# A gathered block's input fetched half a block ahead, its residual mid-way, and the final norms of the dense blocks interleaved

## The chip, the cores and the metric

The kernel runs on one core of a Trainium2 chip. The core has five engines with instruction streams of their own: TensorE (PE, matrix products into PSUM), VectorE (DVE), ScalarE (ACT), GpSimd (POOL) and SyncE (SP), which here only issues DMAs. The metric is the device time of one execution in microseconds. It is read from three runs of the kernel before: a median of 2697.93 us (2694.83 to 2700.26).

## The reference, cut to what matters

One layer of a streaming encoder over 1024 tokens of width 1024, in float32. A token mixer comes first (not touched here). Then follows a retrieval over 128 x 128 = 16384 single-neuron experts, and a final norm:

```python
def peer_ffn(x, wq, k1, k2, u_tab, v_tab):
    def block(xb):                      # 128 tokens
        ...                             # 8 heads, each picks its 16 best experts: e, softmax weights g
        u_sel = u_tab[e]
        act = jax.nn.gelu(jnp.einsum('thkd,td->thk', u_sel, xb))
        v_sel = v_tab[e]
        return jnp.einsum('thk,thkd->td', g * act, v_sel)
...
    h = h + peer_ffn(rms_norm(h, norm2_g[l]), ...)
return rms_norm(h, normf_g)             # x * rsqrt(mean(x*x) + 1e-6) * g
```

Each token uses 8 x 16 = 128 experts. Per block of 128 tokens one can gather the 128 rows of `u_tab` and of `v_tab` that each token needs, or multiply with all 16384 experts and weigh by a mostly zero matrix.

## The kernel before, in words

The eight token blocks are divided: five (numbers 0 to 4, `ND`) go the dense way on PE, three (`NG`) the gathered way on DVE, at the same time.

**Dense blocks.** `first` computes gelu(u x) for one column of 128 experts and all 640 tokens (tiles `ap`, `aa`, `ha`); 97 such columns are computed ahead and stored to the DRAM tensor `A_d`. The weights are built as `G_d` and loaded as `gt`. The loop `dense` then goes over 32 groups of four columns. In each it loads `hr` (from `A_d`), `vr` and `ur`, weighs (`weigh`), splits values into a high and a low part (`hh`, `hl`, `vh`, `vl`, `uh`, `ul`; high on ACT, low on DVE) and multiplies on PE: 24 matmuls of width 512 for each token block. Blocks 0 to 3 go to accumulators `vp` (PSUM, two buffers, taken by `pair`) and are added to the residual on DVE by `add`; block 4 stays in the accumulator `total` over all groups. The next buffer of `vp` is free only when its `add` is done.

**Gathered blocks.** `gather(n)` is a generator. It loads the block's normalized input `xg` from DRAM (`X_d`) and forms 128 dot products on DVE, one for each gathered row of `u` (the instruction shown as CUSTOM_DVE, `row<-row,xg`). Then it loads the residual `hb` (from `H_d`), applies gelu, and adds 128 weighted rows of `v` to it (SCALAR_TENSOR_TENSOR, `hb<-row,act,hb`). `finish` norms the result and stores it. Rows are gathered by POOL into a ring of eight buffers; `xg`, `hb` and `act` have one buffer each.

**What sets the order.** In front of the dense loop a planner (`Merge`) interleaves generators by estimated costs, and the scheduler of the language places DMAs on SP where their buffers come free. The dense loop is written out by hand (`manual_schedule`): `rows_of(slot)` draws a fixed share of gathered rows at seven places of each group. SP issues in program order, so a DMA that waits holds back all later ones.

**The end.** The last group does block 0 and block 1; then `last` does blocks 2, 3 and 4. Each block's `finish` norms it: a square with a sum on ACT, a root on ACT, five one-column operations on DVE (`rsqrt_cols`), a load of the norm's weights `nf` for all partitions, one multiply on DVE and one store.

Most instructions are recorded through a helper and carry its line, 146; they are told apart by their tiles. DMA issues carry their own lines: 1254 `xg`, 1262 `hb`, 1278 `nf`, 1283 the output, 1318 `hr`, 1322 `vr`, 1382 the store of `A_d`, 1424 `gt`.

Of the kernel before, what the change touches and what calls it, by code (L numbers as in the profile page):

```python
# [7 lines left out]
F32 = mybir.dt.float32  # L8
# [939 lines left out]
def peer(tc, a, cst, pools, h, nx, mg):  # L948
# [299 lines left out]
    def gate():  # L1248
        return (lambda: mg.units < share[0]) if share else None

    def gather(n):

        xg = gp.tile([P, D], F32, name="xg", tag="xg", bufs=1)
        nc.sync.dma_start(xg, X_d[n])
        act = gp.tile([P, P], F32, name="act", tag="act", bufs=1)
        for k in range(P):
            ub = take()
            yield gate()
            V.tensor_tensor_reduce(ub, ub, xg, 1.0, 0.0, ALU.mult, ALU.add, act[:, k:k + 1])
            mg.units += 1  # L1260
        hb = gp.tile([P, D], F32, name="hb", tag="hb", bufs=1)
        nc.sync.dma_start(hb, H_d[n])
        S.activation(act, act, AF.Gelu_apprx_tanh)
        yield
        V.tensor_tensor(act, act, gw[n], ALU.mult)
        yield
        for k in range(P):
            vb = take()
            yield gate()
            V.scalar_tensor_tensor(hb, vb, act[:, k:k + 1], hb, ALU.mult, ALU.add)  # L1270
            mg.units += 1
        finish(ND + n, hb)
        yield
# [172 lines left out]
        while mg.units < 2 * NG * P and left - (2 * NG * P - mg.units) + 1 <= spread[0]:  # L1446
            row()

    def second(p_, b, t, first, last):
        bs = slice(b * P, b * P + P)  # L1450
        for i in range(2):
            ns = slice(512 * i, 512 * i + 512)
            PE.matmul(p_[:, i], t.hh[:, bs], t.vl[:, ns], start=first, stop=False)
            PE.matmul(p_[:, i], t.hl[:, bs], t.vh[:, ns], start=False, stop=False)
# [5 lines left out]
    def pair():  # L1460
        return ppv.tile([P, 2, 512], F32, name="vp", tag="vp")
# [72 lines left out]
    def dense():  # L1534
# [3 lines left out]
        for c in range(nch):  # L1538
# [32 lines left out]
                second(pr[1], 1, t, jj == 0, jj == JC - 1)  # L1571
            add(0, pr[0])
            if not more:
                finish(0, acc[0])
            rows_of(2)
            if not more:
                last(now, pr)
                return

            pr.append(pair())  # L1580
            for jj, t in enumerate(now):
# [33 lines left out]

    def last(now, pr):

        for b in (2, 3, 4):
            p_ = pair() if b < 4 else total
            for jj, t in enumerate(now):  # L1620
                second(p_, b, t, b < 4 and jj == 0, jj == JC - 1)
            if b == 2:
                add(1, pr[1])
                finish(1, acc[1])
            else:
                add(b - 1, p0)
                finish(b - 1, acc[b - 1])
            p0 = p_
        add(4, total)
        finish(4, acc[4])  # L1630

    with tc.manual_schedule():
        dense()
# [81 lines left out]
```

## Time and profile before

| what | value |
|---|---|
| median of three runs | 2697.93 us (2694.83 to 2700.26) |
| the profiled execution's own time | 2685.19 us |
| its span, first to last instruction | 2683.4 us |
| mean granted PE clock | 0.974 |
| busy: PE, DVE, ACT, POOL | 94%, 88%, 50%, 44% of the span |
| DMA | 755.39 MB, mean 282 GB/s |

The span has three parts: the mixer and the choice of experts (to about 700 us), the building of the weights beside the columns computed ahead (to about 1550 us), and the dense loop with its end. In a row of the timeline stand the start in us, the duration, the engine, the operation with its output and inputs, and in brackets the idle time before it with what ended it. Rows `PE` are matmuls, whose ends are modelled. In a chain's row stand the start, the length and what was waited for or done.

### The profile page before, as it was taken

How to read it: one execution, taken by the hardware profiler on the slowest of the kernel's cores; microseconds unless marked ns; L12 is line 12 of the kernel's file. 1: busy time of each engine (PE TensorE's matmuls, PEld its weight loads, DVE VectorE, ACT ScalarE, POOL GpSimd, SP SyncE). 2: the span in 40 equal slices, each digit the busy share in tenths (PEclk: the TensorE clock that was granted, in tenths of full speed). 3: DMA queues.
4: the chain of work that ended last, by engine and by line, in shares of the span. 5: the costliest groups of instructions: out<-in, count | busy, mean ns of one | idle time of the engine just before them, and what ended most of it. 6: DMA issues, size and time to landing. Idle time of an engine off the chain costs nothing.

```text
span 2683.4 us, 40720 instructions
## 1 busy us (share of the span) xinstructions
PE 2517.4 (94%) x14623; PEld 2276.8 (85%) x14623; DVE 2364.5 (88%) x4541; ACT 1330.2 (50%) x2408; POOL 1172.7 (44%) x777
## 2 busy tenths in 40 slices
PE   5989899998999999999899889999899999999997
PEld 5766688998999999999899878888788888888885
DVE  6888649998999999999899779999888888999996
ACT  5457524322693965938739544444334333333432
POOL 0000000155573767847637535554444545555440
PEclk9989899999999999999999899999999999999998
DMA  5111324488899998999989989999899999999993
GB/s 169 32 35 37 126 80 127 147 281 313 275 401 317 354 392 306 396 341 357 401 276 364 388 321 331 332 328 323 291 329 326 330 324 329 333 329 327 329 330 133
DMA packets 298250, 755.39 MB, mean 282 GB/s; under 512 B 28352, under 2 KB 122752, under 8 KB 293312
## 3 DMA queue, kind: packets, MB, share of 16 engines
q0 software_dynamic: 110592, 402.70, 41.6%
q1 hardware_dynamic: 180720, 338.90, 35.6%
q10 hardware_dynamic: 6736, 11.19, 1.2%
q8 instruction: 115, 1.88, 0.3%
q14 instruction: 87, 0.71, 0.1%
HBM read 665.54 MB, written 85.98 MB: 280 GB/s over the span
## 4 chain that ended last, share of the span: by engine, by line
PE 60%; DVE 21%; DMA 9%; ACT 6%; issue 4%; ACTq 0%; SPq 0%; POOL 0%; DVEq 0%; POOLq 0%
PE vp L146 25%; PE ap L146 17%; PE total L146 6%; DMA A_d<-aa 4%; PE qp L146 4%; ACT ohB L146 3%; PE gp L146 3%; PE wop L146 3%; DVE row L146 2%; DVE oh L146 2%; DVE ul L146 2%; PE pj L146 2%; DVE hb L146 1%; DVE ix L146 1%; DMA nf<-in_gf_dram 1%
## 5 line engine op out<-in xcount | busy, mean ns | idle before, releaser
L1233 POOL DMA_INDIRECT row<-in_peer_u_dram,idx x384 | 562.6, 1465 | 961.0 <-DVE scv L146 495.6
L1233 POOL DMA_INDIRECT row<-in_peer_v_dram,idx x384 | 607.3, 1581 | 448.0 <-DVE hb L146 328.8
L146 PE MATMUL ap<-xDl,uh 128*128 128x320 f32 x2048 | 655.4, 320 | 30.5 <-ACT aa L146 23.9
L146 PE MATMUL ap<-xDh,ul 128*128 128x320 f32 x2048 | 648.0, 316 | 8.5 <-DVE ul L146 8.5
L146 PE MATMUL ap<-xDh,uh 128*128 128x320 f32 x2048 | 645.8, 315 | 0.0
L146 DVE SCALAR_TENSOR_TENSOR hb<-row,act,hb 128x1024 f32<-128x1024 f32 x384 | 492.3, 1282 | 8.9 <-DMA row<-in_peer_v_dram,idx 4.5
L146 DVE CUSTOM_DVE_ANT_0 row<-row,xg 128x1024 f32<-128x1024 f32 x384 | 458.4, 1219 | 15.4 <-DMA row<-in_peer_u_dram,idx 7.8
L146 PEld LDWEIGHTS ap<-xDl,uh 128*128 128x128 f32 x2048 | 392.5, 192 | 34.7 <-ACT aa L146 26.5
L146 PE MATMUL vp<-vl,hh 128*128 128x512 f32 x1024 | 400.7, 391 | 12.4 <-DVE vl L146 10.8
L146 PEld LDWEIGHTS ap<-xDh,ul 128*128 128x128 f32 x2048 | 392.3, 192 | 12.2 <-DVE ul L146 10.6
L146 PE MATMUL vp<-vh,hl 128*128 128x512 f32 x1024 | 399.9, 391 | 0.0
L146 PE MATMUL vp<-vh,hh 128*128 128x512 f32 x1024 | 399.6, 390 | 0.0
L146 PEld LDWEIGHTS ap<-xDh,uh 128*128 128x128 f32 x2048 | 391.7, 191 | 0.0
L146 ACT ACTIVATE gq<-gt 128x640 f32<-128x640 f32 x128 | 175.1, 1368 | 330.9 <-DVE hr L146 325.2
L146 DVE TENSOR_TENSOR ul<-ur,uh 128x1024 fp32r<-128x1024 f32 x128 | 155.9, 1218 | 97.3 <-ACT uh L146 97.2
L146 PEld LDWEIGHTS vp<-vl,hh 128*128 128x128 f32 x1024 | 193.0, 189 | 53.4 <-DVE vl L146 11.6
L146 PEld LDWEIGHTS vp<-vh,hh 128*128 128x128 f32 x1024 | 193.1, 189 | 40.5
L146 PEld LDWEIGHTS vp<-vh,hl 128*128 128x128 f32 x1024 | 193.2, 189 | 38.8
L146 PE MATMUL gp<-ohB,ohA 128*128 128x128 f32 x1280 | 198.1, 281 | 18.8 <-ACT gs L146 12.0
L146 ACT ACTIVATE aa<-ap 128x320 f32<-128x320 f32 x194 | 84.5, 437 | 258.8 <-PE ap L146 207.0
L146 ACT ACTIVATE ohB<-ohB,kt 128x128 f32<-128x128 f32 x480 | 204.4, 497 | 0.0
L146 PEld LDWEIGHTS gp<-ohB,ohA 128*128 128x128 f32 x1280 | 179.7, 193 | 24.4 <-ACT gs L146 13.3
(440 smaller groups left out, 4498.3 us busy)
## 6 DMA issues: line engine op xcount, KB each, us to landing
ur<-in_uT_dram SPq DMA_DIRECT2D x128, 512.0 KB, 6.7
vr<-in_peer_v_dram SPq DMA_DIRECT2D x128, 512.0 KB, 6.2
gt<-G_d SPq DMA_DIRECT2D x32, 1280.0 KB, 9.7
G_d<-gs SPq DMA_DIRECT2D x19, 2048.0 KB, 25.6
A_d<-aa SPq DMA_DIRECT2D x96, 320.0 KB, 8.6
hr<-A_d SPq DMA_DIRECT2D x96, 320.0 KB, 5.9
wqr<-in_wq_dram SPq DMA_DIRECT2D x31, 512.0 KB, 3.9
row<-in_peer_u_dram,idx POOLq DMA_INDIRECT x384, 7.2
```

What stands on the lines that cost most here:

```text
L146: return fn(*args, **kw)
L1233: G.indirect_dma_start(out=r, out_offset=None, in_=a["peer_v" if at >= P else "peer_u"], in_offset=bass.IndirectOffsetOnAxis(ap=idx[n][:, ...
```

## The change

Two separate edits.

In `gather`, the input `xg` of block n + 1 is fetched right behind the 128 dot products of block n, half a block ahead of its use, and handed over in a list; only block 0 still fetches its own. The residual `hb` is fetched behind the 65th dot product of its block, not behind the last.

In `last`, the norms of the five dense blocks become generators which are advanced in turns. The norm's weights `nf` are loaded once. The square of block b (ACT) is issued as soon as block b is added, and the rest of block b's norm comes after the next block's addition. Block 4's matmuls are issued by halves of the output: all of the first 512 columns, then all of the second. Its addition, its square (now on DVE, with a running sum) and its last multiply and store are done by halves. The last multiply of block 3 and its store come after those of block 4.

```diff
     def gather(n):
-        xg = gp.tile([P, D], F32, name="xg", tag="xg", bufs=1)
-        nc.sync.dma_start(xg, X_d[n])
+        xg = fetch_xg(n) if n == 0 else held.pop()
         act = gp.tile([P, P], F32, name="act", tag="act", bufs=1)
         for k in range(P):
             ub = take()
             yield gate()
             V.tensor_tensor_reduce(ub, ub, xg, 1.0, 0.0, ALU.mult, ALU.add, act[:, k:k + 1])
             mg.units += 1
-        hb = gp.tile([P, D], F32, name="hb", tag="hb", bufs=1)
-        nc.sync.dma_start(hb, H_d[n])
+            if k == P // 2:
+                hb = gp.tile([P, D], F32, name="hb", tag="hb", bufs=1)
+                nc.sync.dma_start(hb, H_d[n])
+        if n + 1 < NG:
+            held.append(fetch_xg(n + 1))
         S.activation(act, act, AF.Gelu_apprx_tanh)
...
-    def second(p_, b, t, first, last):
+    def second(p_, b, t, first, last, halves=(0, 1)):
         bs = slice(b * P, b * P + P)
-        for i in range(2):
+        for i in halves:
...
             add(0, pr[0])
             if not more:
-                finish(0, acc[0])
-            rows_of(2)
-            if not more:
                 last(now, pr)
                 return
+            rows_of(2)
...
     def last(now, pr):
+        nf = rows.tile([P, D], F32, name="nf", tag="row")
+        nc.sync.dma_start(nf, a["gf"].partition_broadcast(P))
+        def norm(b):
+            st = gp.tile([P, 5], F32, name="st4", tag="st4", bufs=2)
+            sq = rows.tile([P, D], F32, name="sqf", tag="row")
+            x = acc[b]
+            if b < 4:
+                S.activation(sq, x, AF.Square, accum_out=st[:, 2:3])
+                yield
+            else:
+                for i in range(2):
+                    xi = x[:, 512 * i:512 * i + 512]
+                    V.tensor_tensor(xi, xi, total[:, i], ALU.add)
+                    V.tensor_tensor_reduce(sq[:, 512 * i:512 * i + 512], xi, xi, 1.0, 0.0, ALU.mult, ALU.add,
+                                           st[:, i:i + 1])
+                    yield
+                V.tensor_tensor(st[:, 2:3], st[:, 0:1], st[:, 1:2], ALU.add)
+            v, dst = st[:, 3:4], st[:, 4:5]
+            V.tensor_scalar(v, st[:, 2:3], 1.0 / D, EPS, ALU.mult, ALU.add)
+            S.activation(dst, v, AF.Sqrt)
+            yield
+            V.reciprocal(dst, dst)
...
+            yield
+            n = 1 if b < 4 else 2
+            for i in range(n):
+                ns = slice(D // n * i, D // n * (i + 1))
+                V.scalar_tensor_tensor(x[:, ns], x[:, ns], dst, nf[:, ns], ALU.mult, ALU.mult)
+                nc.sync.dma_start(out_v[:, b, ns], x[:, ns])
+        g = [norm(b) for b in range(5)]
+        next(g[0])
+        rows_of(2)
+        p0 = pr[1]
+        for b in (2, 3):
+            p_ = pair()
             for jj, t in enumerate(now):
...
+            add(b - 1, p0)
+            next(g[b - 1])
+            for _ in g[b - 2]:
+                pass
             p0 = p_
+        for jj, t in enumerate(now):
+            second(total, 4, t, False, jj == JC - 1, (0,))
+        add(3, p0)
+        next(g[3])
+        for _ in g[2]:
+            pass
+        for jj, t in enumerate(now):
+            second(total, 4, t, False, jj == JC - 1, (1,))
+        next(g[4])
+        next(g[3])
+        next(g[4])
+        next(g[4])
+        next(g[3])
+        next(g[4])
+        for n in (4, 3):
+            for _ in g[n]:
+                pass
```

How the instructions move, at three places.

SP at the opening of the dense loop, where the last stores of `A_d` and `G_d` and the first loads of the loop are issued. Before:

```order
L1288 DMA ur<-in_uT_dram 128x1024
L1382 DMA A_d<-aa 128x640
L1322 DMA vr<-in_peer_v_dram 128x1024
L1188 DMA G_d<-gs 128x128
L1188 DMA G_d<-gs 128x31x128
L1424 DMA gt<-G_d 128x2560
```

With the change:

```order
L1297 DMA ur<-in_uT_dram 128x1024
L1391 DMA A_d<-aa 128x640
L1255 DMA xg<-X_d 128x1024
L1331 DMA vr<-in_peer_v_dram 128x1024
L1188 DMA G_d<-gs 128x128
L1188 DMA G_d<-gs 128x31x128
L1433 DMA gt<-G_d 128x2560
```

This fetch is the third gathered block's. It is the one of the three whose place on SP changes: the first two stand where they stood. Of the three loads of `hb`, only the third block's has moved, too.

SP at the boundary between the second and the third gathered block, in the dense loop. Before:

```order
L1278 DMA nf<-in_gf_dram 128x1024
L1283 DMA out_dram<-hb 128x1024
L1424 DMA gt<-G_d 128x2560
L1322 DMA vr<-in_peer_v_dram 128x1024
L1318 DMA hr<-A_d 128x640
L1254 DMA xg<-X_d 128x1024
L1322 DMA vr<-in_peer_v_dram 128x1024 x2
```

With the change:

```order
L1287 DMA nf<-in_gf_dram 128x1024
L1292 DMA out_dram<-hb 128x1024
L1433 DMA gt<-G_d 128x2560
L1331 DMA vr<-in_peer_v_dram 128x1024
L1327 DMA hr<-A_d 128x640
L1331 DMA vr<-in_peer_v_dram 128x1024 x2
```

The fetch is gone from here; the others keep their order.

DVE at the very end (h_2454 is the residual of dense block 3, h_2455 that of block 4; the numbered `st` are the columns of one block's norm: st_25310 of block 3, st_25334 of block 4; an ISA row of width 512 is the product with a running sum). Before, block 4 after all of block 3:

```order
L146 SCALAR_TENSOR_TENSOR h_2454<-h_2454,st,nf 128x1024
L146 TENSOR_TENSOR h_2455<-h_2455,total 128x1024
L146 TENSOR_SCALAR st<-st 128x1
L146 RECIPROCAL st<-st 128x1
L146 TENSOR_TENSOR st<-st 128x1 x2
L146 TENSOR_SCALAR st<-st 128x1
L146 TENSOR_TENSOR st<-st 128x1
L146 SCALAR_TENSOR_TENSOR h_2455<-h_2455,st,nf 128x1024
```

With the change, from block 4's first half on, up to the first reciprocal:

```order
L146 TENSOR_TENSOR h_2455<-h_2455,total 128x512
L146 ISA sqf,st_25334<-h_2455 128x512
L146 ISA st_25334 128x1
L146 TENSOR_SCALAR st_25310<-st_25310 128x1
L146 TENSOR_TENSOR h_2455<-h_2455,total 128x512
L146 ISA sqf,st_25334<-h_2455 128x512
L146 ISA st_25334 128x1
L146 TENSOR_TENSOR st_25334<-st_25334 128x1
L146 TENSOR_SCALAR st_25334<-st_25334 128x1
L146 RECIPROCAL st_25310<-st_25310 128x1
```

The norms of blocks 3 and 4 now share this stretch; behind it come the remaining columns of both, the two half multiplies of block 4 and the multiply of block 3.

More of the change, by code (lines that the diff above doesn't have):

```diff
@@ L1249, in gate, with fetch_xg, gather @@
         return (lambda: mg.units < share[0]) if share else None
-    def gather(n):
+    held = []
+    def fetch_xg(n):
         xg = gp.tile([P, D], F32, name="xg", tag="xg", bufs=1)
         nc.sync.dma_start(xg, X_d[n])
+        return xg
+    def gather(n):
+        xg = fetch_xg(n) if n == 0 else held.pop()
         act = gp.tile([P, P], F32, name="act", tag="act", bufs=1)
@@ L1616, in last @@
     def last(now, pr):
-        for b in (2, 3, 4):
-            p_ = pair() if b < 4 else total
-            for jj, t in enumerate(now):
[L1621 to L1627, printed above, removed]
-            p0 = p_
-        add(4, total)
-        finish(4, acc[4])
+        nf = rows.tile([P, D], F32, name="nf", tag="row")
@@ new lines, in last @@
+        nc.sync.dma_start(nf, a["gf"].partition_broadcast(P))
[19 more added lines that the diff above has]
+            V.reciprocal(dst, dst)
+            V.tensor_tensor(v, v, dst, ALU.mult)
+            V.tensor_tensor(v, v, dst, ALU.mult)
+            V.tensor_scalar(v, v, -0.5, 1.5, ALU.mult, ALU.add)
+            V.tensor_tensor(dst, dst, v, ALU.mult)
+            yield
[4 more added lines that the diff above has]
+                nc.sync.dma_start(out_v[:, b, ns], x[:, ns])
@@ new lines, in last @@
+        g = [norm(b) for b in range(5)]
[4 more added lines that the diff above has]
+            p_ = pair()
+            for jj, t in enumerate(now):
+                second(p_, b, t, jj == 0, jj == JC - 1)
+            add(b - 1, p0)
+            next(g[b - 1])
+            for _ in g[b - 2]:
+                pass
+            p0 = p_
+        for jj, t in enumerate(now):
+            second(total, 4, t, False, jj == JC - 1, (0,))
+        add(3, p0)
```

## The prediction

> **What bounds the kernel now.** I read the page first, then the busy time by stretches, then the timeline and the chain of waits at the three places that the change touches. On the page, the engine totals:
>
> ```profile
> PE 2517.4 (94%) x14623; PEld 2276.8 (85%) x14623; DVE 2364.5 (88%) x4541; ACT 1330.2 (50%) x2408; POOL 1172.7 (44%) x777
> ```
>
> PE and DVE are both near full, so an edit is worth something only where PE stands still and cannot make it up. Inside the dense loop it never does. One group of four expert columns, in a table by stretches (length, then busy PE, PEld, DVE, ACT, POOL, the granted clock, DMA share, GB/s):
>
> ```profile
> 1963.60:1997.86 34.26, 34.26 (x169) 29.58 (x169) 30.39 (x42) 13.75 (x15) 16.42 (x13) 1.00 0.91 327
> ```
>
> PE is busy 34.26 of 34.26 us while DVE has almost 4 us free. A stall of PE is therefore lost to the end, and a PE second saved early in the loop comes out at the end. The places to price are: the boundary between the second and third gathered block (1912 us), the opening of the dense loop (1510 to 1552 us), where the early fetch lands, and the tail after the last products (from 2648 us).
>
> **Part 1, the boundary: the input is already there.** Timeline of DVE, PE and the chain around it:
>
> ```profile
> 1902.99 0.31 PE L146 MATMUL ap<-xDl,uh 128*128 128x320 f32 x1
> 1911.18 0.82 DVE L146 TENSOR_TENSOR hl<-hr,hh 128x640 fp32r<-128x640 f32 x1
> 1912.39 6.75 DMA xg<-X_d
> 1919.28 1.22 DVE L146 CUSTOM_DVE_ANT_0 row<-row,xg 128x1024 f32<-128x1024 f32 x1 [7.28 <-DMA xg<-X_d]
> 1921.58 1.22 DVE L146 TENSOR_TENSOR vl<-vr,vh 128x1024 fp32r<-128x1024 f32 x1
> 1922.85 0.79 PE L146 MATMUL vp<-vl,hh 128*128 128x512 f32 x1 [8.57 <-DVE vl L146]
> 1932.10 1.22 DVE L146 TENSOR_TENSOR h<-h,vp 128x1024 f32<-128x1024 f32 x1 [0.17 <-PE vp L146]
> 1948.22 0.31 PE L146 MATMUL ap<-xDl,uh 128*128 128x320 f32 x1
> 1982.47 0.31 PE L146 MATMUL ap<-xDl,uh 128*128 128x320 f32 x1
> ```
>
> The fetch is issued only when the block before is finished, takes 6.75 us, and DVE stands 7.28 us at the first dot product. Queued behind that product on DVE is the split `vl`, for which PE waits 8.57 us. From the first `ap` of this group to that of the next it is 1948.22 - 1902.99 = 45.23 us; a regular group takes 1982.47 - 1948.22 = 34.25. So the boundary costs PE 10.98 us: 8.57 of idle time and 2.41 more, because PE comes back slow:
>
> ```profile
> 1923.00:1926.00 3.00, 3.00 (x7) 0.50 0.89 302
> ```
>
> (PE alone here: 7 matmuls in 3 us at a granted clock of 0.50.) With the input in place DVE runs on, and `vl` ends 7.28 us earlier, at 1915.5. PE, idle since 1914.28, then waits 1.29 us and should keep its clock. That would be a gain of 10.98 - 1.29 - 0.2 for the restart = 9.5. DVE allows a little less. Its addition at 1932.10 waits 0.17 us for PE now; moved up it starts at 1932.10 - 0.17 - 7.28 = 1924.65 and frees its accumulator at 1925.87. PE, with 42 matmuls (6 left of block 0, 24 of block 1, 12 of blocks 2 and 4) at 0.227 us between its restart and that accumulator (0.227: 23 steps from 2661.55 to 2666.76, rows below), is there at 1915.5 + 0.2 + 9.5 = 1925.2 and waits about 0.7. Gain: 9.5 - 0.7 = **8.7 us**. Bounds: 7.28 (DVE's shift alone) and 9.5. The gathered rows, asked for on POOL, are not late:
>
> ```profile
> 1908.13 0.94 POOL L1233 DMA_INDIRECT row<-in_peer_u_dram,idx  x1 [3.84 <-DVE hb L146]
> 1920.78 1.68 POOL L1233 DMA_INDIRECT row<-in_peer_u_dram,idx  x1 [11.71 <-DVE act L146]
> ```
>
> The eighth row of the third block is asked for at 1908.13, before the boundary; the ninth waits for the first dot product to free a buffer and moves up with it.
>
> Does 1.29 us keep the clock? Two other idle times of PE, each with the stretch behind it:
>
> ```profile
> 2639.91 0.50 PE L146 MATMUL vp<-vl,hh 128*128 128x512 f32 x1 [2.20 <-DVE vl L146]
> 2649.86 0.50 PE L146 MATMUL vp<-vl,hh 128*128 128x512 f32 x1 [1.23 <-DVE h L146]
> 2640.00:2643.00 3.00, 3.00 (x9) 0.62 0.00 0
> 2650.00:2653.00 3.00, 3.00 (x14) 1.00 0.88 291
> ```
>
> After 2.20 us the clock fell to 0.62, after 1.23 us it stayed at 1.00; 1.29 is next to the second. The Trainium skill, "TensorE: Matmul & The Clock Gate", section "What's actually happening", has the clock halve after an idle window of about 3.4 us in a free-running count. By that the remaining gap is harmless too, but 2.20 us should have been as well, and the trace says it was not; so the rule alone is no safeguard.
>
> **Part 2, the opening: where the fetch goes.** The order of SP puts the third block's input between a store of `A_d` and the load of `vr` at the opening. The issue waits there for the last dot product of the second block (the buffer is single), and all later loads and stores stand behind it on SP.
>
> ```profile
> 1508.80 0.08 DVE L146 DVE_READ_ACCUMULATOR2_ANT act<- 128x1 f32 x1
> 1516.51 1.17 SPq L1322 DMA_DIRECT2D vr<-in_peer_v_dram  x1
> 1544.01 6.17 DMA hr<-A_d
> 1550.28 0.96 PE L146 MATMUL ap<-xDl,uh 128*128 128x320 f32 x2 [6.61 <-ACT uh L146]
> 1516.00:1550.00 34.00, 16.80 (x96) 16.27 (x96) 9.56 (x8) 7.59 (x11) 7.18 (x7) 0.78 1.04 382
> q0 software_dynamic: 110592, 402.70, 41.6%
> q1 hardware_dynamic: 180720, 338.90, 35.6%
> xg<-X_d SPq DMA_DIRECT2D x3, 512.0 KB, 6.8
> ```
>
> The product is done at 1508.88 and SP comes by at 1516.5, so it does not wait. But the DMA engines are full (share 1.04, 382 GB/s) and PE waits for what lies behind (`hr`, `ur`): the 512 KB that cost nothing to carry at 1912 push these back. At the full 382 GB/s that is 524 / 382 = 1.37 us; where gathers (q0) and SP's transfers (q1) halve the rate, as their like shares suggest, 2.74 us. Bounds: 0 and the transfer's own landing time, 6.8. Fewer bytes elsewhere cannot make the opening faster. I take the middle of the two rates, **+2.1 us**.
>
> The residual `hb` of the third block also moves, half a block up. Nobody waits for it now and nobody will: 0. The first and second block's fetches keep their rows on SP: 0.
>
> **Part 3, the tail.** Rows of DVE, ACT, PE and SP, the chain's row for the norm weights, and one 512-wide DVE operation for scale:
>
> ```profile
> 2646.42 0.16 DVE L146 RECIPROCAL st<-st 128x1 f32<-128x1 f32 x1 [1.36 <-ACT st L146]
> 2647.39 1.28 DVE L146 SCALAR_TENSOR_TENSOR hb<-hb,st,nf 128x1024 f32<-128x1024 f32 x1
> 2648.59 1.21 DVE L146 TENSOR_TENSOR h<-h,vp 128x1024 f32<-128x1024 f32 x1
> 2649.84 1.06 ACT L146 ACTIVATE sqf<-h 128x1024 f32<-128x1024 f32 x1 [3.45 <-DVE h L146]
> 2653.51 1.28 DVE L146 SCALAR_TENSOR_TENSOR h<-h,st,nf 128x1024 f32<-128x1024 f32 x1 [1.12 <-DMA nf<-in_gf_dram]
> 2655.98 0.50 PE L146 MATMUL vp<-vl,hh 128*128 128x512 f32 x1 [0.38 <-DVE h L146]
> 2661.55 0.39 PE L146 MATMUL total<-vl,hh 128*128 128x512 f32 x1
> 2666.76 0.39 PE L146 MATMUL total<-vh,hh 128*128 128x512 f32 x1
> 2673.29 1.21 DVE L146 TENSOR_TENSOR h<-h,total 128x1024 f32<-128x1024 f32 x1
> 2673.85 4.37 DMA nf<-in_gf_dram
> 2675.77 0.15 DVE L146 TENSOR_SCALAR st<-st 128x1 f32<-128x1 f32 x1 [1.26 <-ACT sqf L146]
> 2678.31 1.28 DVE L146 SCALAR_TENSOR_TENSOR h<-h,st,nf 128x1024 f32<-128x1024 f32 x1 [1.18 <-DMA nf<-in_gf_dram]
> 2679.62 0.34 SPq L1283 DMA_DIRECT2D out_dram<-h  x1
> 1502.50 0.69 DVE L146 TENSOR_TENSOR ohA<-iota,kt 128x512 f32<-128x512 f32 x1
> ```
>
> PE's last matmul starts at 2666.76; 13 us later the last output leaves. The five dense norms run one after the other, each with its own load of the same weights, issued behind the store before it: store, load (4.37 us), multiply, store. From the last multiply's end, 2679.59, to the span's end (2683.4) it is 3.8 us.
>
> Now in the new order. A full-width DVE operation frees the engine after 1.14 (addition) or 1.20 us (multiply), one of half width after 0.61, a one-column one after 0.19; reciprocal to multiply is 0.97 (the two first rows); a square is 1.25 on ACT. The addition of block 0 stays at 2648.59; block 1's follows at 2649.73, so PE no longer stops at 2655.98 and ends 0.54 earlier: block 3 at 2661.2, block 4's halves at 2663.9 and 2666.6. The one load still sits behind the third gathered block's store, so block 0's multiply stays at 2653.51. Block 2's addition waits for PE, 2655.65 to 2656.8; block 1's root stands behind block 2's square on ACT, 2658.15, its multiply runs 2659.4 to 2660.6. Block 3's addition starts at 2661.2; block 2's root comes behind block 3's square, 2663.65, its multiply runs 2664.9 to 2666.1. From there DVE is not idle: half addition 0.61, half product 0.66, one column 0.19 (2667.5), the second half's 0.61 and 0.66, two columns 0.38 (2669.2), reciprocals of block 3 (0.97) and block 4 (0.97; 2671.1), two half multiplies (1.24; 2672.35), and block 3's multiply, 1.28: 2673.6. That is 2679.6 - 2673.6 = **6.0 us** earlier, with the same 3.8 behind it. Bounds: if a half-width operation cost as much as a whole one, six of them would take 3.6 back (gain 2.4); if DVE had nothing but block 4 behind PE's end and block 3's last multiply, it would end at 2672.1 (gain 7.5).
>
> **Sum:** -8.7 + 2.1 - 6.0 = -12.6 us, that is -0.47%. The profiled execution took 2685.2 us (span 2683.4) and becomes 2672.6. The runs' median, 2697.9, stands 12.7 above that execution, and the trace doesn't show where; I carry the difference over: **2685.3 us**.
>
> **Rivals.**
> 1. *The opening pays the whole landing.* For: full DMA, an in-order SP, and `A_d` written and read back within it. Against: a transfer in a queue overlaps with its neighbours. Cost 6.8 in place of 2.1: -7.9, 2690.0.
> 2. *PE cools anyway* in the 1.29 us left. For: 2.20 us were enough at 2639.91. Against: 1.23 were not. Eight matmuls at 0.43 in place of 0.227 cost 1.6, of which the 0.7 wait for the accumulator hides some: -11.7, 2686.2.
> 3. *Half-width operations cost as whole ones*: -9.0, 2688.9. The 0.69 us of the 512-wide row speaks against it.
> 4. *Another wait takes the place of the one removed*: the third block's first rows come late, and only opening and tail count: -3.9, 2694.0. Against: eight rows were asked for before the boundary.
> 5. *Slower: the fetch holds SP.* If the second block's last product ends later than SP's passage at 1516.5, SP stops, and `vr`, the `G_d` stores, `gt`, `A_d` and `hr` behind it, one us for each us. The margin is 7.6 us; the gains are used up when the product ends 12.6 us after that passage, at 1529. With 18 us it would be 2703.3. For: SP takes its instructions in order, and nothing ties its place to DVE's. Against: here DVE, not SP, is ahead.
>
> **How the numbers follow.** Chances: forecast 0.55, rival 1 0.17, rival 2 0.10, rival 3 0.08, rival 4 0.07, rival 5 0.03. The three runs lie 2694.8 to 2700.3, so a median moves by some 2.5 us; about 0.2%, 5.4 us, is what can be told from no change. The forecast's own range is 2681 to 2689.5; with rivals 1 to 3 it is 2679.5 to 2692. Faster needs a time below 2692.5: nearly all of forecast and rivals 2 and 3 (0.70), four fifths of rival 1 and a little of rival 4: 0.85. Same: the rest of these, 0.12. Slower: 0.03.
>
> **What would show it.** Right: no wait for `xg` at the boundary, a PE gap of 1 to 2 us there at clock 1.00, the boundary group near 36.5 us; PE's first full group some 2 us later after the opening; one `nf` load in the tail, the last multiply about 7 us behind the last matmul. Wrong: a wait of SP at the early fetch, a PE gap in the opening longer by 5 us or more, row waits after the boundary, or half-width rows above 1 us.

## The result, and the profile after

Six executions of the changed kernel have a median of 2679.1 us (2669.1 to 2681.0), against 2699.1 (2690.1 to 2704.9) before; the ratio is 0.9934, interval [0.9911, 0.9957]. In a second comparison, twelve executions of the same change (below, "the change once more") gave 0.9969 [0.9943, 0.9994]. Weighting the two by their intervals gives 0.9950, plus or minus 0.0017: 13.6 us less, give or take 4.6. Forecast were 12.6 less (0.9953) and 2685.3 us.

The profiled execution took 2669.1 us (span 2667.4), 16.0 of span less than the profile before. Not all of that is the change's: the profile after is already 3.6 us ahead at the end of the second gathered block, before the third block's input is fetched, and a second profile of the same program is 10.5 us behind there. So two places are used below as marks: the product `act<-act,gw` on DVE that follows the second gathered block's last dot product (M), and the first `ap` of the loop's second full group (G). M to G is the **opening**; G to the span's end is the **rest**, in which the boundary and the tail lie. The marks before and after, DVE and PE timelines:

```profile
1510.03 0.29 DVE L146 TENSOR_TENSOR act<-act,gw 128x128 f32<-128x128 f32 x1
1594.77 0.31 PE L146 MATMUL ap<-xDl,uh 128*128 128x320 f32 x1
```

```profile
1506.43 0.28 DVE L146 TENSOR_TENSOR act<-act,gw 128x128 f32<-128x128 f32 x1
1590.73 0.31 PE L146 MATMUL ap<-xDl,uh 128*128 128x320 f32 x1
```

Before: opening 84.74, rest 2683.4 - 1594.77 = 1088.6. After: opening 84.30, rest 2667.4 - 1590.73 = 1076.7. The rest is 12.0 us shorter. In the second profile of the change (span 2675.7, G at 1599.42) the rest is 1076.3. The two profiles of one program differ by 8.3 us in their span and by 0.4 in the rest, so most of what differs from run to run lies ahead of G. That the rest agrees so closely is in part chance: the second profile's boundary group is 0.97 us longer and its last group 1.33 us shorter (table below). So a part of the rest is read to 1 or 1.5 us, which is still far better than the runs can tell.

**The boundary.** The group around it after the change, PE and DVE timelines, and two rows of the table by stretches (its columns as in the prediction):

```profile
1899.49 0.31 PE L146 MATMUL ap<-xDl,uh 128*128 128x320 f32 x1
1906.70 0.82 DVE L146 TENSOR_TENSOR hl<-hr,hh 128x640 fp32r<-128x640 f32 x1
1907.44 1.22 DVE L146 CUSTOM_DVE_ANT_0 row<-row,xg 128x1024 f32<-128x1024 f32 x1
1909.73 1.22 DVE L146 TENSOR_TENSOR vl<-vr,vh 128x1024 fp32r<-128x1024 f32 x1
1911.00 0.50 PE L146 MATMUL vp<-vl,hh 128*128 128x512 f32 x1 [0.17 <-DVE vl L146]
1921.27 0.50 PE L146 MATMUL vp<-vl,hh 128*128 128x512 f32 x1 [0.46 <-DVE h L146]
1935.01 0.31 PE L146 MATMUL ap<-xDl,uh 128*128 128x320 f32 x1
```

```profile
1899.49:1935.01 35.52, 34.90 (x169) 29.42 (x168) 33.38 (x50) 16.51 (x20) 20.20 (x14) 1.00 0.92 339
1935.01:1969.32 34.31, 34.31 (x170) 29.57 (x168) 30.37 (x42) 13.75 (x15) 16.47 (x13) 1.00 0.93 336
```

DVE starts the first dot product right behind `hl`, with no wait for `xg`. PE's wait for `vl` falls from 8.57 us to 0.17, the addition that frees its accumulator holds it for 0.46, and the clock is 1.00 throughout. The group takes 1935.01 - 1899.49 = 35.52 us, 1.21 more than the regular one behind it, where it was 10.98 more before: 9.8 us gained.

**The opening.** The fetch on SP after the change, what the fetch waited for in the second profile (a row of SP's waits: total, times, longest), and PE's longest wait in the opening, after and before:

```profile
1506.79 0.38 SPq L1255 DMA_DIRECT2D xg<-X_d  x1
```

```profile
SPq L1255 <- DVE act L146: 0.9, 1, 0.9
```

```profile
1541.94 0.64 PE L146 MATMUL ap<-xDl,uh 128*128 128x320 f32 x1 [16.01 <-ACT aa L146]
```

```profile
1526.54 0.64 PE L146 MATMUL ap<-xDl,uh 128*128 128x320 f32 x1 [10.90 <-ACT aa L146]
```

In the profile after, the fetch is issued in 0.38 us and does not hold SP. In the second profile SP came to it first and waited 0.9 us for the last dot product of the second block. PE's longest wait is 5.1 us longer after than before, which by itself was one of the forecast's signs of being wrong. But it is a shift between waits: PE's idle time from M to G is 18.9 us before, 19.5 after and 15.6 in the second profile.

**The tail.** PE, DVE and SP timelines after the change:

```profile
2627.90 0.50 PE L146 MATMUL vp<-vl,hh 128*128 128x512 f32 x1 [2.19 <-DVE vl L146]
2637.86 0.80 PE L146 MATMUL vp<-vl,hh 128*128 128x512 f32 x1 [2.86 <-DVE h L146]
2655.42 0.39 PE L146 MATMUL total<-vh,hh 128*128 128x512 f32 x1
```

```profile
2636.59 2.35 DVE L146 TENSOR_TENSOR h<-h,vp 128x1024 f32<-128x1024 f32 x2
2644.97 1.22 DVE L146 TENSOR_TENSOR h<-h,vp 128x1024 f32<-128x1024 f32 x1 [2.13 <-PE vp L146]
2650.41 1.22 DVE L146 TENSOR_TENSOR h<-h,vp 128x1024 f32<-128x1024 f32 x1 [0.61 <-PE vp L146]
2655.84 0.69 DVE L146 TENSOR_TENSOR h<-h,total 128x512 f32<-128x512 f32 x1 [0.60 <-PE total L146]
2660.76 2.61 DVE L146 SCALAR_TENSOR_TENSOR h<-h,st,nf 128x512 f32<-128x512 f32 x3
```

```profile
2637.13 0.38 SPq L1626 DMA_DIRECT2D nf<-in_gf_dram  x1
```

One `nf` load; the additions of blocks 0 and 1 stand together (x2). From the first addition to the end of the last multiply it is 2663.37 - 2636.59 = 26.8 us, where it was 31.0: 4.2 gained, not 6.0. From PE's last matmul to that end it is 7.95 us, where it was 12.83. Three things in these rows were not in the forecast. PE kept its clock over the 2.19 us at 2627.90 (before, 2.20 us had cooled it), so block 1 ended earlier and PE waited 2.86 us for the first addition, not 1.23. Behind that wait it was slow:

```profile
2638.00:2641.00 3.00, 3.00 (x8) 2.38 (x9) 1.73 (x6) 2.21 (x5) 0.00 (x0) 0.53 0.93 291
```

so block 2's addition waited 2.13 us for PE. And the first half of block 4 waits 0.60 us for `total`, though PE had started the last matmul of that half 12 matmuls, or 2.7 us, before that of the whole.

The rest adds up: 9.8 (boundary) + 4.2 (last group, 80.68 to 76.53) - 0.2 behind the last multiply = 13.8 gained; measured were 12.0. The missing 1.8 us are in the regular groups: 34.31 in place of 34.25 (29 steps of it, 1.7 us). That was not in the forecast either.

### The profile page after: what moved, and what is told of

Read it like the earlier page. It is cut to its first block, busy times and chain, and to the rows that moved or that the text cites. A ratio compares the mean times of both kernels' runs of the same rounds, so it can differ in the third digit from the quotient of the medians.

```text
span 2667.4 us, 40711 instructions
## 1 busy us (share of the span) xinstructions
PE 2510.3 (94%) x14623; PEld 2269.9 (85%) x14623; DVE 2364.8 (89%) x4548; ACT 1326.7 (50%) x2406; POOL 1162.8 (44%) x777
## 4 chain that ended last, share of the span: by engine, by line
PE 55%; DVE 21%; DMA 12%; ACT 6%; issue 4%; POOL 1%; SPq 0%; ACTq 0%; DVEq 0%; POOLq 0%
PE vp L146 25%; PE ap L146 14%; DMA A_d<-aa 8%; PE total L146 6%; ACT ohB L146 3%; PE wop L146 3%; DVE oh L146 2%; DVE row L146 2%; DVE ul L146 2%; PE gp L146 2%; PE pj L146 2%; DMA ur<-in_uT_dram 2%; PE qp L146 2%; DVE hb L146 1%; DVE ci L146 1%
## 5 line engine op out<-in xcount | busy, mean ns | idle before, releaser
L1233 POOL DMA_INDIRECT row<-in_peer_u_dram,idx x384 | 571.2, 1487 | 939.6 <-DVE scv L146 493.9
L1233 POOL DMA_INDIRECT row<-in_peer_v_dram,idx x384 | 588.9, 1533 | 467.6 <-DVE hb L146 345.0
```

The source lines that it names most:

```text
L1233: G.indirect_dma_start(out=r, out_offset=None, in_=a["peer_v" if at >= P else "peer_u"], in_offset=bass.IndirectOffsetOnAxis(ap=idx[n][:, ...
```

## The experiments

The theory: the boundary gives 9 to 10 us, the tail 4 to 6, the opening takes at most 2. The rivals: the fetch costs the opening its whole landing; the gain of the tail is not the interleaving but something else in it. In each diff, lines with - and + are against the kernel before or after, as said.

Experiments 1 to 4 share one comparison (2690.6 us before), 5 to 8 another (2693.0). All profiles by the marks (us; "last group" is from its first `ap` to the end of the last multiply):

```
kernel              fetch in    M       opening  regular  boundary  last    rest
                    opening                      group    group     group
before              no       1510.03    84.74    34.25    45.23     80.68   1088.6
after               yes      1506.43    84.30    34.31    35.52     76.53   1076.7
the change again    yes      1520.54    78.88    34.31    36.49     75.20   1076.3
1 fetch only        yes      1517.09    78.89    34.25    35.52     80.53   1078.8
2 tail only         no       1514.51    78.46    34.31    44.85     76.63   1086.0
3 fetch in loop     no       1520.48    79.76    34.31    35.57     75.21   1075.4
4 one nf load       no       1525.94    78.69    34.25    43.84     76.25   1082.6
5 total in two      yes      1520.46    84.03    34.31    35.51     74.48   1074.6
6 block 4 whole     yes      1509.86    84.51    34.31    35.51     77.96   1077.6
7 four more         yes + 4  1524.46    85.42    34.31    36.54     78.01   1078.9
8 no gap            yes      1521.27    85.67    34.27    35.52     68.94   1067.5
8 no gap again      yes      1527.29    82.29    34.27    36.04     68.92   1067.9
9 no gap, in loop   no       1534.40    78.08    34.27    35.56     68.91   1067.5
```

**1. The fetch alone.** Against before:

```diff
...
+        xg = fetch_xg(n) if n == 0 else held.pop()
...
+            if k == P // 2:
+                hb = gp.tile([P, D], F32, name="hb", tag="hb", bufs=1)
+                nc.sync.dma_start(hb, H_d[n])
+        if n + 1 < NG:
+            held.append(fetch_xg(n + 1))
```

> The kernel before with the edits of gather alone (the input fetched half a block ahead, the residual mid-way); the tail is that of before. Theory A, the terms as the trace of the change has them: the boundary group takes 35 to 37 us instead of 45.2 (a gain of 8 to 9.5), PE's idle time in the opening grows by 0 to 3 us, the tail from the addition of block 0 to the last multiply stays at 31.0 us; time -6 to -9 us. Rival B, most of the measured 18 us comes from the tail or from somewhere that neither edit touches: -3 us or less here.

Measured: 2682.0 against 2690.6 us, ratio 0.9970 [0.9953, 0.9987]; the rest is 9.8 us shorter. PE's timeline at the boundary:

```profile
1915.72 0.50 PE L146 MATMUL vp<-vl,hh 128*128 128x512 f32 x1 [0.23 <-DVE vl L146]
1925.99 0.50 PE L146 MATMUL vp<-vl,hh 128*128 128x512 f32 x1 [0.42 <-DVE h L146]
```

The same two waits as in the change: the boundary's gain is the fetch's alone, and the last group (80.53) is that of before.

**2. The tail alone.** Against before: the whole of the change except `fetch_xg`, `held` and the place of `hb`.

> The kernel before with the edits of last alone (norms interleaved, block 4 by halves); the gathered blocks fetch as before. Theory A: the boundary still costs 45 us for its group with a wait of some 7 us for the input; the tail from the addition of block 0 to the end of the last multiply takes 25 to 27 us instead of 31.0; time -4 to -6 us. Rival B: -10 us or more here.

Measured: 2684.4 us, ratio 0.9982 [0.9964, 1.0001], no difference that these runs can tell; the rest is 2.6 us shorter. The last group gains 4.05 us, the regular groups lose 1.7. At the boundary DVE and PE wait as before:

```profile
1917.90 1.23 DVE L146 CUSTOM_DVE_ANT_0 row<-row,xg 128x1024 f32<-128x1024 f32 x1 [7.55 <-DMA xg<-X_d]
1921.47 0.80 PE L146 MATMUL vp<-vl,hh 128*128 128x512 f32 x1 [8.39 <-DVE vl L146]
```

The two halves of the change add, as far as these runs can tell: 0.30% + 0.18% = 0.48%, each known to about 0.18, against 0.50% for both. By the rest it is 9.8 + 2.6 = 12.4 us, against 12.0 and 12.4.

**3. The third block's input fetched in the loop**, not in the opening. Against after:

```diff
-        if n + 1 < NG:
-            held.append(fetch_xg(n + 1))
+        if n == 0:
+            held.append(fetch_xg(1))
...
+            if n == 1 and k == P // 2:
+                held.append(fetch_xg(2))
```

> The changed kernel, but the third block's input is fetched behind the 65th weighted row of the second block, some 150 us later, inside the dense loop, and no longer in the opening. The buffer is free there. Theory A (the fetch costs the opening 0.6 to 2 us, and nothing in the loop): no wait for the input at the boundary, the boundary group at 35 to 37 us, PE's idle time in the opening back to about 19 us as before, time 0 to 2 us below the changed kernel, which the times cannot tell apart from it. Rival (the opening pays the whole landing of 6.8 us, or more through what stands behind it): 5 us or more below the changed kernel. Other rival (the loop's transfers have no room): PE waits appear in the loop at the fetch.

Measured: 2676.1 us, ratio 0.9954 [0.9937, 0.9972]; opening 79.76, boundary 35.57. PE's idle time in the opening is 14.5 us, not the 19 expected; the paragraph on the openings below has why this proves little. The fetch is as good for the boundary half a block later. Beside the change's two comparisons (0.9934, 0.9969) the fetch in the opening shows no cost that these times can tell.

Its tail tells something else. PE timeline, and its stretch behind the wait:

```profile
2637.45 0.50 PE L146 MATMUL vp<-vl,hh 128*128 128x512 f32 x1 [2.22 <-DVE vl L146]
2647.41 0.50 PE L146 MATMUL vp<-vl,hh 128*128 128x512 f32 x1 [2.87 <-DVE h L146]
```

```profile
2648.00:2651.00 3.00, 3.00 (x15) 2.47 (x14) 1.44 (x7) 1.76 (x5) 0.00 (x0) 1.00 0.79 229
```

The same two waits, 2.22 and 2.87 us, and the clock is 1.00 behind both. The last group is 1.3 us shorter for it (75.21 against 76.53).

**4. One load of `nf`, nothing else.** Against before:

```diff
...
+        if one:
+            nf = one[0]
+        else:
             nf = rows.tile([P, D], F32, name="nf", tag="row")
             nc.sync.dma_start(nf, a["gf"].partition_broadcast(P))
+        if b == 0:
+            one.append(nf)
```

> The kernel before with one edit: the dense blocks' norms use one load of the norm weights instead of five; order, widths and everything else as before. If the serial loads of 4.4 us are what the tail of before consists of, four of the five waits of 1.05 to 1.2 us vanish and nothing more: the stretch from the addition of block 0 to the last multiply goes from 31.0 to about 26.5 us (4 x 1.15), which would be as much as the whole interleaving with halves brought (26.8 in the trace of the change). If the interleaving is what counts, it stays above 29.

Measured: 2686.0 us, ratio 0.9981 [0.9966, 0.9996]; last group 76.25, which is 4.43 us shorter than before, as much as the whole new tail gave in the profile after (4.15). The last rows of DVE, and PE's last matmul:

```profile
2677.28 1.29 DVE L146 SCALAR_TENSOR_TENSOR h<-h,st,nf 128x1024 f32<-128x1024 f32 x1
2678.48 1.22 DVE L146 TENSOR_TENSOR h<-h,total 128x1024 f32<-128x1024 f32 x1
2682.35 1.28 DVE L146 SCALAR_TENSOR_TENSOR h<-h,st,nf 128x1024 f32<-128x1024 f32 x1
```

```profile
2675.35 0.39 PE L146 MATMUL total<-vh,hh 128*128 128x512 f32 x1
```

From that matmul to the last multiply's end it is 8.28 us, against 12.83 before and 7.95 in the change. The norms still run one after the other here. So most of the tail's gain is that four norms no longer wait for a load of weights that were on the chip already. PE cools behind its first wait here, as before and in the second profile of the change, where the last group gains 5.48 us; of that the one load has four fifths. By the rest this edit alone gains 6.0 us (1.4 of it at the boundary, which it does not touch), more than the whole new tail of experiment 2 with 2.6: the regular groups keep their 34.25 us here, and PE's clock does not fall at the wait where it fell in experiment 2.

**5. The accumulator `total` in two tiles**, one for each half. Against after:

```diff
-    total = ppr.tile([P, 2, 512], F32, name="total")
+    total = [ppr.tile([P, 512], F32, name=f"total{i}") for i in range(2)]
...
-                    V.tensor_tensor(xi, xi, total[:, i], ALU.add)
+                    V.tensor_tensor(xi, xi, total[i], ALU.add)
```

> The changed kernel with one edit: block 4's accumulator is two tiles, one for each half of the output, so that the addition of the first half can wait for the first half's matmuls alone. In the trace of the change that addition waits 0.60 us for PE and starts only when the second half's matmuls end, as if it waited for both halves. If the one tile is the cause, that wait is gone, the addition starts when DVE comes to it, and the tail from the addition of block 0 to the last multiply is about 0.6 us shorter (26.2 us, or 24.9 if PE keeps its clock there). If it is PE itself that is late, the wait stays. The time as a whole can't tell 0.6 us.

Measured: 2681.5 against 2693.0 us, ratio 0.9956 [0.9933, 0.9979]. DVE and PE timelines:

```profile
2657.37 1.22 DVE L146 TENSOR_TENSOR h<-h,vp 128x1024 f32<-128x1024 f32 x1 [0.76 <-PE vp L146]
2667.56 0.68 DVE L146 TENSOR_TENSOR h<-h,total 128x512 f32<-128x512 f32 x1
```

```profile
2651.59 0.50 PE L146 MATMUL vp<-vl,hh 128*128 128x512 f32 x1 [2.86 <-DVE h L146]
```

The half's wait of 0.60 us is gone. PE's clock held behind both its waits here; against experiment 3, where it held too, with one tile, the last group is 0.73 us shorter (74.48 against 75.21). With one tile the first half's addition waited for the matmuls of the second half.

**6. Block 4 whole**, norms interleaved as in the change. Against after:

```diff
...
-            second(total, 4, t, False, jj == JC - 1, (0,))
+            second(total, 4, t, False, jj == JC - 1)
...
-        for jj, t in enumerate(now):
-            second(total, 4, t, False, jj == JC - 1, (1,))
+        add(4, total)
...
```

> The changed kernel, with block 4 not by halves: its matmuls, its addition, its square (on ACT again), its multiply and its store are whole; norms still interleaved, one load of the norm weights, block 3's norm ahead of block 4's. Worth of the halves by the rows: with them, from the first half's addition to the last multiply's end 7.5 us; without, addition 1.2, square 1.27, root 0.42, four columns 0.97, multiply 1.28 is 5.1 us behind PE's end, beside which block 3's 2.2 us of columns and multiply can run. So the tail from the addition of block 0 to the last multiply should be 0 to 2.5 us shorter than the change's 26.8, not longer, if the halves bring nothing; 1 us or more longer if they do.

Measured: 2681.6 us, ratio 0.9956 [0.9933, 0.9979]. From PE's last matmul to the last multiply's end it is 7.83 us, where the halves have 7.95: as they stand, the halves bring nothing. Taken by itself the last group (77.96, 1.4 us longer than in the profile after) would say that they do bring something. But PE lost its clock behind the same wait as there, and for 6.8 us in place of 3.4. Experiment 7 keeps the halves, lost its clock at this wait for 6.8 us too, and its last group takes 78.01. PE's wait in experiment 6:

```profile
2641.48 0.79 PE L146 MATMUL vp<-vl,hh 128*128 128x512 f32 x1 [2.85 <-DVE h L146]
```

**7. Four more transfers in the opening.** After the second gathered block, four stores of 512 KB each go from a row buffer to memory that nobody reads. Against after:

```diff
...
+        if n == 1:
+            for i in range(4):
+                nc.sync.dma_start(E_d[i], ub)
```

> The changed kernel, with four more transfers of 512 KB each (a row tile to a scratch tensor in DRAM, not used) in the opening of the dense loop beside the early fetch, each after the last dot product of the second block; some loads of the opening trade places on SP by it. It multiplies the disputed cost of the fetch by five. If the opening is bound by the DMA engines and a transfer there costs 1.4 to 2.7 us as the prediction had it, the time rises by 5.5 to 11 us over the change and so does PE's idle time between 1500 and 1570 us. If transfers there have room (0.6 us or nothing each), it rises by less than 3 us.

Measured: 2686.3 us, ratio 0.9977 [0.9961, 0.9993]. That is 4.8 us more than experiments 5 and 6 of the same comparison, 1.2 us for each transfer; it lies between the two expectations, and the intervals overlap, so it is a size and no proof. The opening is 85.42, near those of four profiles with one fetch (84.03 to 85.67), and PE's idle time in it is 18.6 us, not more than the 19.5 of the profile after. What the four cost, if they cost, is small beside the 6.75 us that one such fetch took to land at the boundary before.

**8. No gap in the last group.** What the rows above showed, taken together: `total` in two tiles; the split `vl` of the last products ahead of the gathered rows on DVE; the third gathered block's norm among the others; `nf` and ACT's table for the root (a load of 1.28 us) loaded at the start of the last group; each norm's last part behind the next block's addition. Against after, its core:

```diff
+            if not more:
+                nf = rows.tile([P, D], F32, name="nf", tag="row")
+                nc.sync.dma_start(nf, a["gf"].partition_broadcast(P))
+                S.activation(warm, cst["iota"][:, 0:1], AF.Sqrt)
+                now[3].low_v()
             rows_of(0)
-            now[3].low_v()
+            if more:
+                now[3].low_v()
...
+        if n == NG - 1:
+            held.append(hb)
+        else:
+            finish(ND + n, hb)
...
+        next(g7)
+        add(0, pr[0])
+        next(g[0])
+        next(g7)
```

> A version that follows the traces: the change with block 4's accumulator in two tiles; in the last group the split of v comes ahead of the gathered rows, the third gathered block's norm is no longer done ahead of block 0's addition but is one of the interleaved norms, the norm weights are loaded once, at the start of the last group, and the table of the root is loaded early by a root of one column. If the two waits of PE in the tail (2.2 us for the split, 2.9 us for block 0's addition behind the third block's norm, with its slow clock behind them) are what is left, both vanish, PE's last matmul comes some 6 us earlier, and the time is 6 to 9 us below the change (about -1.0% against the kernel before). If DVE is then the bound, the gain is smaller, and DVE has no idle time in the tail.

Measured: 2670.5 us, ratio 0.9921 [0.9891, 0.9950]; last group 68.94, 11.7 us shorter than before. DVE, and the only wait of PE:

```profile
2640.30 6.56 DVE L146 SCALAR_TENSOR_TENSOR hb<-row,act,hb 128x1024 f32<-128x1024 f32 x5
2646.77 1.21 DVE L146 TENSOR_TENSOR h<-h,vp 128x1024 f32<-128x1024 f32 x1
2664.73 0.69 DVE L146 TENSOR_TENSOR h<-h,total 128x512 f32<-128x512 f32 x1 [1.23 <-PE total L146]
2668.26 2.61 DVE L146 SCALAR_TENSOR_TENSOR h<-h,st,nf 128x512 f32<-128x512 f32 x3
```

```profile
2648.04 0.50 PE L146 MATMUL vp<-vl,hh 128*128 128x512 f32 x1 [0.51 <-DVE h L146]
```

Both waits of over 2 us are gone, and in this group PE's clock is 1.00 up to its last matmul.

**The change once more, and the last version with and without the fetch in the opening,** in one comparison. The change is as it was, and so is the version of experiment 8; the third kernel is that version with the edit of experiment 3.

> The change itself once more, beside the two versions of the last comparison, so that they share the runs of the kernel before. Theory (boundary 9 us gained, tail 4 to 6 us, opening at most 2 us lost): ratio 0.9945 to 0.9960, 11 to 15 us less. If the first result (0.9934) held a gain that the two edits don't explain, the ratio is again below 0.994.

> The version without the gaps of the last group, with the fetch in the opening, beside the change. By the trace its last group is 7.5 us shorter than the change's (33.58 against 41.13): 7 to 8 us faster than the change, ratio 0.9915 to 0.9935. If the clock's loss in the tail of the change was of that one profiled run alone, 5 us.

> The version without the gaps of the last group, with the third gathered block's input fetched inside the loop (behind the 65th v row of the second block) and not in the opening. If the early fetch costs the opening the 2.1 us of the forecast, this is 2 us (0.0008) faster than the same version with the fetch in the opening; if it costs the whole landing, 7 us (0.0025); by the theory that the fetch costs the opening nothing that can be seen, the same to 1 us: 6 to 8 us below the change, ratio 0.9915 to 0.9935.

Measured against 2692.1 us: the change 2684.5, 0.9969 [0.9943, 0.9994]; no gap 2675.4, 0.9922 [0.9898, 0.9946]; no gap with the fetch in the loop 2670.9, 0.9899 [0.9873, 0.9925]. The change came out above its expected ratio (0.9945 to 0.9960) and the third kernel below its own (0.9915 to 0.9935), each with an interval that reaches into it. The third is the best kernel of the study, about 1% below the one before. In the second profile of the change PE cooled at the first wait and not at the second. PE timeline and the two stretches, in the order of time:

```profile
2637.55 0.50 PE L146 MATMUL vp<-vl,hh 128*128 128x512 f32 x1 [2.24 <-DVE vl L146]
2647.51 0.50 PE L146 MATMUL vp<-vl,hh 128*128 128x512 f32 x1 [1.24 <-DVE h L146]
```

```profile
2638.00:2641.00 3.00, 3.00 (x11) 2.34 (x10) 2.93 (x3) 0.00 (x0) 0.00 (x0) 0.65 0.00 0
```

```profile
2648.00:2651.00 3.00, 3.00 (x15) 2.47 (x14) 1.53 (x7) 1.86 (x5) 0.00 (x0) 1.00 0.79 246
```

The slow block 1 fills most of the second wait (1.24 in place of 2.86), as in the profile before, and the last group takes 75.20.

With the fetch in the opening, the seven openings average 82.65 us (experiment 7 left out), without it five average 79.95. The difference is 2.7 us, but each group scatters by 2.75 us (standard deviation), so the interval is -0.9 to 6.3. The kernels differ in other ways as well. The openings fall in two clumps, 78 to 80 and 82 to 86, and both kinds of kernel have members in both: the change itself has 84.30 and 78.88, the kernels without the fetch 84.74 and 78.08. In the short clump PE stands idle for 14.5 to 15.7 us of the opening, in the long one for 16.5 to 19.5. What decides the clump wasn't found.

## Why the prediction was right

**The boundary, -8.7 forecast, -9.8 measured** in the profile after and -9.7 in experiments 1 and 3; -8.8 in the second profile of the change (36.49 - 34.31 = 2.18 left of 10.98). The steps held: no wait at the dot product, PE's gap no longer than 1.29 us, the clock kept, a short wait for the accumulator (0.46 us, not 0.7). What makes the two sizes is a wait that the forecast took as given, that of the second block's own norm for its `nf`, on DVE ahead of the split `vl`. Before, in the second profile of the change, and in the profile after:

```profile
1906.58 1.28 DVE L146 SCALAR_TENSOR_TENSOR hb<-hb,st,nf 128x1024 f32<-128x1024 f32 x1 [1.01 <-DMA nf<-in_gf_dram]
```

```profile
1911.77 1.28 DVE L146 SCALAR_TENSOR_TENSOR hb<-hb,st,nf 128x1024 f32<-128x1024 f32 x1 [1.00 <-DMA nf<-in_gf_dram]
1920.66 0.50 PE L146 MATMUL vp<-vl,hh 128*128 128x512 f32 x1 [1.13 <-DVE vl L146]
```

```profile
1902.10 1.28 DVE L146 SCALAR_TENSOR_TENSOR hb<-hb,st,nf 128x1024 f32<-128x1024 f32 x1
```

With that wait PE's gap is 1.13 us, near the 1.29, and the gain 8.8, the forecast's value. Without it the gap is 0.17 and the gain 9.8, beyond the upper bound of 9.5, which let the wait stand.

**The opening, +2.1 forecast**: the runs allow it and do not settle it. By the openings of the profiles it is +2.7 [-0.9, 6.3]; by experiment 7 1.2 for each transfer; by the last comparison 4.5 us between medians whose intervals overlap. Zero is not excluded.

**The tail, -6.0 forecast; -4.2 and -5.5 measured.** The step that was mis-sized is PE at block 0's addition: the forecast took over from the profile before that PE cools at the wait ahead of it and then waits only 1.23 us here. Which of the two waits cools PE changes from run to run (see the last section). From that addition to block 2's, the forecast has 7.06 us; the second profile has 2653.28 - 2646.24 = 7.04, the profile after 2644.97 - 2636.59 = 8.38: its clock fell behind block 0's addition, worth 1.3 us. Where it does not fall, 0.5 to 0.6 us are left, and experiment 5 shows them: the half of `total` that waits for both. With that gone, and the clock kept, the addition of block 0 to the last multiply's end takes 24.75 us; the forecast was 25.0. That the parts were right does not make the reason right. The forecast priced the new order as a whole and gave the single load no term of its own; experiment 4 has 4.4 us from the one load alone, and experiment 6 nothing from the halves.

**A term that was missing**: +1.7 us for the regular groups, in every kernel with the tail of the change (34.31; 34.27 in the kernels 8 and 9 of the table), and not in experiments 1 and 4 (34.25). It is a property of the program, not of the run: both profiles of the change have it.

**The move of `hb`**, forecast 0: no instruction waits for its load in the profile after.

**The sum**: 12.6 less forecast; by the two comparisons 13.6, give or take 4.6. The rest is the stricter test, and there the forecast, without its opening, had 14.7 less; measured are 12.0 and 12.4. The boundary gave 1.1 and 0.1 us more than forecast, the tail 1.8 and 0.5 less, the regular groups cost 1.7 and the end behind the last multiply 0.2. So the steps held, but their sum without the opening is some 2.5 us too high. Whether the opening takes its 2.1 us stays open; that the total of 12.6 lies so near the measured 13.6 is therefore partly luck. The time itself, 2685.3, was carried from the first runs' median; the median after is 6.2 below it, also just below the forecast's own range (2681 to 2689.5), and the second comparison's is 0.8 below it.

**The rivals.** 1, the whole landing of 6.8 in the opening: just outside the interval of the profiles, and against experiment 7. 2, PE cools in the gap that is left at the boundary: no, 1.00 in both profiles of the change. It does cool, but in the tail. 3, half-width operations as dear as whole ones: no, the three multiplies at 2660.76 (two half, one whole) take 2.61. 4, the rows come late: no, no row behind the boundary waits. 5, the fetch holds SP: hardly. The margin of 7.6 us, read from SP's passage in the profile before, is not there: in the seven profiles with one fetch in the opening SP comes to it between 3.2 us after the last dot product and 0.9 us before it, and in three of them (experiment 1, the second of the change and the second of experiment 8) it waits 0.9 us.

## What to carry to other kernels

Before a chain is interleaved, look for what each link loads again: one load in place of five gave four fifths of what the whole rewriting of the tail gave. A consumer of half an accumulator was early here only when that half was a tile of its own (0.60 us). And where runs scatter by 10 us, lay two marks in the trace, one behind the noisy stretch and one at the end: the stretch between them agreed within 0.4 us over two executions, its parts within 1.3, and told what the medians could not.

## What was not expected of the hardware

PE's clock falls or stays over one and the same gap. Behind 2.19 to 2.24 us it fell (0.62 and 0.65) in the profile before and in the second of the change, and stayed in the profile after and in experiment 3; behind 2.86 it fell in the profile after (0.53 in its stretch), behind 2.87 it stayed in experiment 3. Gaps up to 1.28 us never lowered it in these profiles. In none of them did it fall at both waits of the tail. Falling at the second cost 1.3 us where the clock stayed down for 3.4 us, and 2.8 where it stayed down for 6.8 (experiments 6 and 7, against 75.21 in experiment 3). The Trainium skill, "TensorE: Matmul & The Clock Gate", section "What's actually happening", has a window of about 3.4 us that runs free of the kernel, so that the moment of a change differs from run to run. That the same gap falls or stays, and the step of 3.413 us shown below, agree with that; that 2.2 us are enough does not agree with a whole idle window of 3.4 us, and here the measurement decides.

The traces show what decides between falling and staying. In each of the thirteen profiles, all changes of the granted clock lie a whole number of steps of 3.413 us apart (to 0.01 us, over the whole execution), a grid that no wait of PE shifts. Behind G, PE has 25 idle times of over 1 us in these profiles, and they divide by how much of one falls between two neighbouring points of its grid. Where that was 2.07 us or more, the clock was halved at the second point (11 times); where it was 1.77 us or less in each step, it stayed (14 times). Ahead of G, where many short waits follow each other, such idle times alone do not tell it: in the second profile of experiment 8 the clock fell behind a step with 1.3 us. Some of those behind G, with the idle time split by the grid (us):

```
profile               idle   split by the grid   clock
after                 2.19   1.43 + 0.76         stays
change, second        2.24   0.17 + 2.07         falls
3 fetch in loop       2.87   1.62 + 1.24         stays
5 total in two        2.86   1.77 + 1.09         stays
after                 2.86   2.38 + 0.48         falls
7 four more           2.86   2.11 + 0.75         falls
```

So a wait of 2 to 3 us costs something or nothing by where it meets the grid, and the 1.3 us by which the tail's two profiles differ is such a chance.

A regular group has the same matmuls in the same order in all kernels, and yet takes 34.25, 34.27 or 34.31 us by program, each to 0.01 over 28 groups. PE timelines of the first product's start in one such group, before and after:

```profile
1670.31 0.39 PE L146 MATMUL vp<-vl,hh 128*128 128x512 f32 x1
1672.58 0.39 PE L146 MATMUL vp<-vh,hl 128*128 128x512 f32 x1
```

```profile
1666.38 0.40 PE L146 MATMUL vp<-vl,hh 128*128 128x512 f32 x1
1668.71 0.39 PE L146 MATMUL vp<-vh,hl 128*128 128x512 f32 x1
```

Ten matmuls take 2.27 us before and 2.33 after; the rest of the group is equal. What does it was not found; no kernel was run for it.
